# Cross-covariance attention: V in 8 KB rows of eight heads, 1 MB loads, and copies of V's transposes that interleave four blocks

## The chip, the cores and the metric

The kernel runs on one core of a Trainium2 chip. The metric is the device time of one execution in microseconds, the median of several runs. The profile is one execution taken by the hardware profiler; its span is a little shorter than the device time.

A core has a matrix engine (TensorE, in the profile PE, with its weight loads as PEld), three engines for elementwise work (VectorE or DVE, ScalarE or ACT, GpSimd or POOL) and a sync engine (SP), which in this kernel issues all transfers. Sixteen DMA engines carry the transfers between the chip's main memory (HBM) and the on-chip memory of 128 partitions (SBUF). TensorE writes its results into a second on-chip memory, PSUM.

## The reference

```python
# Q, K, V: (batch 8, heads 12, seq 512, dim 64), float32
Q_norm = Q / (np.linalg.norm(Q, axis=-2, keepdims=True) + 1e-10)
K_norm = K / (np.linalg.norm(K, axis=-2, keepdims=True) + 1e-10)
attn = np.einsum('bhnd,bhne->bhde', Q_norm, K_norm)        # 64 x 64 per head
attn = np.exp(attn - np.max(attn, axis=-1, keepdims=True))
attn = attn / (np.sum(attn, axis=-1, keepdims=True) + 1e-10)
return np.einsum('bhnd,bhde->bhne', V, attn).astype(np.float32)
```

There are 96 heads. Each head's Q, K and V are 128 KB, and so is its output; in all 37.7 MB are read and 12.6 MB written. The norms run along the sequence, so a head's attention is a 64 x 64 matrix, and everything about Q and K is had from products along the sequence. V is needed with its sequence along the columns of the weights, that is transposed.

## The kernel before

The heads are cut into 24 units of four heads (`U = 24`), and two units make a pair (`S = 12` pairs). A unit's Q lies in 128 partitions of 16 sequence rows each, so that one partition is a contiguous row of 4 KB in HBM, and 32 partitions are one head. Only the last unit's Q and K have another form, two rows of 2 KB per partition.

```python
D, T, HU, J = 64, 16, 4, 8          # dim, sequence rows per partition, heads per unit, T // 2
TAIL, WIDE, BOTH = S - 1, U - 1, S - 8

Qu = Q.rearrange("b h (p t) d -> (b h p) (t d)", t=T)       # rows of 16 x 64 x 4 B = 4 KB
Ku = K.rearrange("b h (p t) d -> (b h p) (t d)", t=T)
Vu = V.rearrange("b h (p t) d -> (b h p) (t d)", t=T)
Of = out.rearrange("b h n d -> (b h n d)").rearrange("(s r i p x) -> s i p r x", r=2, i=2, p=128, x=J * D)

NB = dict(qk=4, v=4, vb=4, qkb=2, vt=2, so=11, sm=2, ab=4)  # buffers of each pool

def load_qk(u, x):                  # x = 0: Q, 1: K; 512 KB each
    if x == 0:
        qk32[u] = qp.tile([128, 2, T, D], F32, name="qk32")
    if u < WIDE:
        nc.sync.dma_start(out=qk32[u][:, x], in_=(Qu, Ku)[x][u * 128:(u + 1) * 128])
    else:
        ...                         # the last unit, rows of 2 KB
def load_v(u):                      # 512 KB
    v32[u] = vp.tile([128, T, D], F32, name="v32")
    nc.sync.dma_start(out=v32[u], in_=Vu[u * 128:(u + 1) * 128])
def store(s, i, k=None):            # 512 KB, rows of 2 KB; the last one in two halves
    ...
    nc.sync.dma_start(out=o[:, :, rows], in_=so[s, i][:, :, rows])
```

The work on a pair: `cast_qk` turns Q and K to bf16 side by side (`qkb`, always VectorE). `grams` multiplies this with itself on TensorE, which gives both the products of Q and K and, on the diagonal, the squared norms (`gram` in PSUM). `squares` and `sums` take the norms (`scr`, `n`), `cross` copies the product of K and Q (`kq`), `powers` takes 1/norm (`r`), `scale_k` scales the rows (`kqs`), `logits` transposes (`lg`), `exps` takes exponentials with the scale of Q and sums them (`ex`, `esum`), `normalise` divides (`ab`).

V goes another way to the same product: `cast_v` (`vb`), `vtrans` (transposes on TensorE into PSUM, `vps`), `vcopy` (to SBUF, `vt`), and then `outs` multiplies with `ab` into PSUM (`po`), `ocopy` copies to `so`, and `store` writes.

```python
def cast_v(eng, u):
    s, r = divmod(u, 2)
    if r == 0:
        vb[s] = vbp.tile([128, T, 2, D], BF16, name="vb")
    copy(eng, vb[s][:, :, r], v32[u])
def vtrans(s, k, c):                # c is None: both blocks of a half in one PSUM tile, 8 transposes
    ...
    for n, c in enumerate(cs):
        for j in range(J // 2):
            t = J * c + k * (J // 2) + j
            nc.tensor.transpose(ps[:, n, j, :], vb[s][:, t].rearrange("p r d -> p (r d)"), identb)
def vcopy(eng, s, k, c):            # two blocks c interleave: c is the innermost of vt
    if k == 0 and not c:
        vt[s] = vtp.tile([128, J, 128, 2], BF16, name="vt")
    o = vt[s][:, k * (J // 2):(k + 1) * (J // 2)].rearrange("p j x c -> p c j x")
    copy(eng, o if c is None else o[:, c:c + 1], vps[s, k, c])
def outs(s, x):                     # 8 products, weights of 64 columns out of vt
    i, k = divmod(x, 2)
    ...
            w = vt[s][:, k * (J // 2) + j, 32 * h:32 * (h + 1), :].rearrange("p x c -> p (x c)")
            nc.tensor.matmul(po[s, x][e * D:(e + 1) * D, j].rearrange("p r d -> p (r d)"), w, ab[s][:, h, :])
```

The order of the instructions on each engine is fixed when the program is built. A small planner (`Order`) lays out all pieces with estimated costs and ranks, and also chooses between engines where two are named (V's casts, `kq`, `kqs`, and from pair `BOTH` on the copies `vt` and `so`). Its ranks are constants of the kernel:

```python
R = dict(cq=4, gr=3.211, sq=1.1, kq=1.1, rd=5.393, pw=2.74, sc=3, rq=1, lg=1.5, ex=1.5, nm=1.394, cv=5, vt=1.1, vc=4.693, ou=1.326, oc=0.6)
BIAS = dict(sc=-0.3, kq=-0.6, cv=-0.3, vc=1, oc=5)
QK_PACE, V_FROM, V_PACE, ST_LAG = 0.5249, 0.1777, 1.0559, 0.6059
```

The sync engine issues transfers in a fixed order, and one waits until the eighth before it has landed.

Of the kernel before, what the change touches and what calls it, by code (L numbers as in the profile page):

```python
# [13 lines left out]
D = 64  # L14
T = 16
# [87 lines left out]
def kernel(  # L103
# [9 lines left out]
    assert N == 32 * T and Q.shape[3] == D  # L113
    U = B * H // HU
    S = U // 2
    TAIL = S - 1
    WIDE = U - 1
    BOTH = S - 8

    Qu = Q.rearrange("b h (p t) d -> (b h p) (t d)", t=T)
    Ku = K.rearrange("b h (p t) d -> (b h p) (t d)", t=T)
    Vu = V.rearrange("b h (p t) d -> (b h p) (t d)", t=T)

    Qw = Q.rearrange("b h (p j) d -> (b h p j d)", j=J).rearrange("(u m p x) -> u p m x", m=2, p=128, x=J * D)
    Kw = K.rearrange("b h (p j) d -> (b h p j d)", j=J).rearrange("(u m p x) -> u p m x", m=2, p=128, x=J * D)

    Of = out.rearrange("b h n d -> (b h n d)").rearrange("(s r i p x) -> s i p r x", r=2, i=2, p=128, x=J * D)

    ctx.enter_context(tc.manual_schedule())

    NB = dict(qk=4, v=4, vb=4, qkb=2, vt=2, so=11, sm=2, ab=4)
    const = ctx.enter_context(tc.tile_pool(name="const", bufs=1))
    qp = ctx.enter_context(tc.tile_pool(name="qp", bufs=NB["qk"]))
    vp = ctx.enter_context(tc.tile_pool(name="vp", bufs=NB["v"]))
# [20 lines left out]
    def copy(eng, o, i):  # L157
        if eng == "ACT":
            nc.scalar.copy(o, i)  # L159
        elif eng == "DVE":  # L160
            nc.vector.tensor_copy(o, i)  # L161
        else:
            nc.gpsimd.tensor_scalar(out=o, in0=i, scalar1=1.0, scalar2=0.0, op0=ALU.mult, op1=ALU.add)  # L163

    def load_qk(u, x):

        if x == 0:
            qk32[u] = qp.tile([128, 2, T, D], F32, name="qk32")
        if u < WIDE:
            nc.sync.dma_start(out=qk32[u][:, x], in_=(Qu, Ku)[x][u * 128:(u + 1) * 128])  # L170
        else:
            nc.sync.dma_start(out=qk32[u][:, x].rearrange("p (m j) d -> p m (j d)", m=2), in_=(Qw, Kw)[x][u])

    def load_v(u):
        v32[u] = vp.tile([128, T, D], F32, name="v32")
        nc.sync.dma_start(out=v32[u], in_=Vu[u * 128:(u + 1) * 128])

    def store(s, i, k=None):
        rows = slice(None) if k is None else slice(k * (J // 2), (k + 1) * (J // 2))
        o = Of[s, i].rearrange("p r (j d) -> p r j d", d=D)  # L180
        nc.sync.dma_start(out=o[:, :, rows], in_=so[s, i][:, :, rows])

    def cast_qk(u, x):
        if x == 0:
            qkb[u] = qkp.tile([128, T, 2 * D], BF16, name="qkb")
        nc.vector.tensor_copy(qkb[u][:, :, x * D:(x + 1) * D], qk32[u][:, x])  # L186

    def cast_v(eng, u):

        s, r = divmod(u, 2)  # L190
        if r == 0:
            vb[s] = vbp.tile([128, T, 2, D], BF16, name="vb")
        copy(eng, vb[s][:, :, r], v32[u])

    def grams(u):

# [69 lines left out]
                out=a[half, :, half], in0=e[half], in1=ri[half, :, None].to_broadcast([D, HU, D]), op=ALU.mult,  # L266
            )

    def vtrans(s, k, c):

        cs = range(2) if c is None else (c,)
        if c is None:
            ps = vps[s, k, c] = ps_v.tile([128, 2, J // 2, 128], BF16, name="vps")
        else:
            ps = vps[s, k, c] = late_pool().tile([128, 1, J // 2, 128], BF16, name="vps")
        for n, c in enumerate(cs):
            for j in range(J // 2):
                t = J * c + k * (J // 2) + j
                nc.tensor.transpose(ps[:, n, j, :], vb[s][:, t].rearrange("p r d -> p (r d)"), identb)  # L279

    def vcopy(eng, s, k, c):
        if k == 0 and not c:
            vt[s] = vtp.tile([128, J, 128, 2], BF16, name="vt")
        o = vt[s][:, k * (J // 2):(k + 1) * (J // 2)].rearrange("p j x c -> p c j x")
        copy(eng, o if c is None else o[:, c:c + 1], vps[s, k, c])

    def outs(s, x):
        i, k = divmod(x, 2)
        po[s, x] = ps_o.tile([128, J // 2, 2, D], F32, name="po")
        for j in range(J // 2):  # L290
            for e in range(2):
                h = 2 * i + e
                w = vt[s][:, k * (J // 2) + j, 32 * h:32 * (h + 1), :].rearrange("p x c -> p (x c)")
                nc.tensor.matmul(po[s, x][e * D:(e + 1) * D, j].rearrange("p r d -> p (r d)"), w, ab[s][:, h, :])  # L294

    def ocopy(eng, s, x):
        i, k = divmod(x, 2)
# [25 lines left out]

    plan = Order(size)
    X = 1.29
    R = dict(cq=4, gr=3.211, sq=1.1, kq=1.1, rd=5.393, pw=2.74, sc=3, rq=1, lg=1.5, ex=1.5, nm=1.394, cv=5, vt=1.1, vc=4.693, ou=1.326, oc=0.6)
    BIAS = dict(sc=-0.3, kq=-0.6, cv=-0.3, vc=1, oc=5)
    QK_PACE, V_FROM, V_PACE, ST_LAG = 0.5249, 0.1777, 1.0559, 0.6059

    def vt_end(s):  # L330
        return ("vt", s, 1, 1 if s >= TAIL else None) if s >= 0 else None

    def v_at(v):
        return V_FROM + V_PACE * v / U
# [7 lines left out]
    def back(kind, i, n, *rest):  # L342
        return (kind, i - n, *rest) if i - n >= 0 else None

    for u in range(U):
        s, r = divmod(u, 2)
        at = QK_PACE * u / U
        free = [back("cq", u, NB["qk"], 0), back("cq", u, NB["qk"], 1)]
        piece(("lq", u), {"DMA": X}, free, [back("lk", u, 1)], at, load_qk, u, 0)
        piece(("lk", u), {"DMA": X}, free, [("lq", u)], at, load_qk, u, 1)  # L350
        piece(("cq", u, 0), {"DVE": 0.72}, [("lq", u), back("gr", u, NB["qkb"])], [back("cq", u, 1, 1)], R["cq"] + 0.01 * u, cast_qk, u, 0)
        piece(("cq", u, 1), {"DVE": 0.72}, [("lk", u)], [("cq", u, 0)], R["cq"] + 0.01 * u, cast_qk, u, 1)
        piece(("gr", u), {"PE": 1.6}, [("cq", u, 0), ("cq", u, 1), back("kq", s, 1)], [back("gr", u, 1)], R["gr"] + 0.01 * u, grams, u)
    for s in range(S):
        SM = NB["sm"]
# [8 lines left out]
        piece(("lg", s), {"PE": 0.6}, [("sc", s), back("ex", s, 1)], [], R["lg"] + 0.01 * s, logits, s)  # L364
        piece(("ex", s), {"ACT": 1.30}, [("lg", s), ("rq", s), back("nm", s, NB["sm"])], [], R["ex"] + 0.01 * s, exps, s)
        piece(("nm", s), {"DVE": 1.12}, [("ex", s)] + [back("ou", s, NB["ab"], x) for x in range(4)], [], R["nm"] + 0.01 * s, normalise, s)
    for v in range(U):
        s = v // 2
        piece(("lv", v), {"DMA": X}, [back("cv", v, NB["v"])], [back("lv", v, 1)], v_at(v), load_v, v)
        piece(("cv", v), {"POOL": 1.15, "DVE": (0.72, BIAS["cv"])} if s >= BOTH else {"POOL": 1.15},  # L370
              [("lv", v), vt_end(v // 2 - NB["vb"])], [back("cv", v, 1)], R["cv"] + 0.01 * v, cast_v, v)
    for s in range(S):
        t = s >= TAIL
        halves = [(k, c) for k in range(2) for c in ((0, 1) if t else (None,))]
        for n, (k, c) in enumerate(halves):
            if not t:
                wait = [("vc", s, 0, None) if k else back("vc", s, 1, 1, None)]
            else:
                wait = [("vc", s - 1, k, c) if s > TAIL else ("kq", S - 1)]
            order = [("vt", s, *halves[n - 1]) if n else ("vt", s - 1, 1, 1 if s > TAIL else None) if s else None]  # L380
            piece(("vt", s, k, c), {"PE": 0.6 if t else 0.8}, [("cv", 2 * s), ("cv", 2 * s + 1)] + wait, order, R["vt"] + 0.01 * s, vtrans, s, k, c)
            order = [("vc", s, *halves[n - 1])] if n else []
            copies = {"ACT": 0.74 if t else 1.31}
            if s >= BOTH:
                copies["DVE"] = (0.74 if t else 1.42, BIAS["vc"])
            piece(("vc", s, k, c), copies, [("vt", s, k, c)] + [back("ou", s, NB["vt"], x) for x in range(4)], order, R["vc"] + 0.01 * s, vcopy, s, k, c)
        for x in range(4):
            i, k = divmod(x, 2)
            n = 4 * s + x - 2
            wait = [("oc", n // 4, n % 4)] if n >= 0 else []  # L390
            order = [("ou", s, x - 1) if x else back("ou", s, 1, 3)]
            piece(("ou", s, x), {"PE": 0.5}, [("vc", s, *h) for h in halves if h[0] == k] + [("nm", s)] + wait, order, R["ou"] + 0.01 * s, outs, s, x)
            n = 2 * s + i - NB["so"]
            free = [("st", n // 2, n % 2)] if k == 0 and n >= 0 else []
            order = [("oc", s, x - 1) if x else back("oc", s, 1, 3)]
            piece(("oc", s, x), {"ACT": 0.6, "DVE": (0.68, BIAS["oc"])} if s >= BOTH else {"ACT": 0.6}, [("ou", s, x)] + free, order, R["oc"] + 0.01 * s, ocopy, s, x)
        for i in range(2):
            order = [("st", s, 0) if i else back("st", s, 1, 1)]
            if (s, i) == (S - 1, 1):

                piece(("sh", s, i), {"DMA": 0.67}, [("oc", s, 2)], order, v_at(2 * s + i) + ST_LAG, store, s, i, 0)
                piece(("st", s, i), {"DMA": 0.67}, [("oc", s, 3)], [("sh", s, i)], v_at(2 * s + i) + ST_LAG, store, s, i, 1)
            else:
                piece(("st", s, i), {"DMA": X}, [("oc", s, 2 * i), ("oc", s, 2 * i + 1)], order, v_at(2 * s + i) + ST_LAG, store, s, i)
# [32 lines left out]
```

## Time and profile before

| | before |
|---|---|
| median of 3 runs | 131.9 us (131.63 to 132.55) |
| span of the profile | 129.5 us |
| transfers issued by the sync engine | 97 (72 loads, 25 stores) |
| busy, VectorE | 94.6 us (73%) |
| busy, TensorE | 78.1 us (60%) |
| busy, ScalarE | 76.8 us (59%) |
| busy, GpSimd | 29.0 us (22%) |

The profile page lists the busy time of each engine, a row of 40 slices for each (a digit is the busy tenth of a slice of 3.2 us, 9 is 90% or more), the DMA queues with their packets, a chain of waits followed back from the last instruction, and the groups of instructions with their mean durations. A line number such as L186 is that of the kernel. "SPq" is the sync engine's queue; a wait such as `SPq L170 <- DMA v<-in_V_dram: 11.5, 13, 1.3` means that issues of line 170 waited 11.5 us in 13 cases, at most 1.3 us, until that transfer had landed.

### The profile page before, as it was taken

Reading aid. Unit: us, or ns where it says so; the run is one execution under the profiler, and the core shown is the slowest. Engines: PE = TensorE matmul, PEld = TensorE weight load, DVE = VectorE, ACT = ScalarE, POOL = GpSimd, SP = SyncE. Lnnn points to the kernel's source line nnn. Section 1 sums busy time; section 2 is a strip of 40 time slices with the busy share of each in tenths; the row PEclk is TensorE's granted clock in tenths of the full one; section 3 lists DMA queues with packets and bytes.
Section 4 is the critical chain, followed back from the end, with each engine's and each line's share of the span. In section 5 each row is a group of like instructions: output and inputs, shape, how many; then the busy total and the mean of one; then the engine's idle time right before and its main releaser. Section 6 shows DMA issues by size and latency. Waiting matters only on the chain.

```text
span 129.5 us, 4929 instructions
## 1 busy us (share of the span) xinstructions
PE 78.1 (60%) x2128; PEld 64.4 (50%) x2128; DVE 94.6 (73%) x148; ACT 76.8 (59%) x218; POOL 29.0 (22%) x33
## 2 busy tenths in 40 slices
PE   0055665955369676864399863596774876678000
PEld 0045654844358464653288752585563765466000
DVE  3445859699898589999938999969999969761000
ACT  3000226690279589994387979168879499598100
POOL 3000090506301191312342033003423030300000
PEclk9999999999955899999756999559999599655555
DMA  3999999999999999999999999999999999999982
GB/s 133 382 410 424 405 412 406 409 406 409 406 410 409 406 406 401 415 402 410 404 403 416 411 414 407 423 409 406 404 413 407 416 397 414 403 405 407 409 331 79
DMA packets 17444, 50.63 MB, mean 391 GB/s; under 512 B 1552, under 2 KB 2064, under 8 KB 17424
## 3 DMA queue, kind: packets, MB, share of 16 engines
q1 hardware_dynamic: 17424, 50.34, 98.3%
q8 instruction: 16, 0.26, 0.8%
q14 instruction: 4, 0.03, 0.1%
HBM read 37.75 MB, written 12.58 MB: 389 GB/s over the span
## 4 chain that ended last, share of the span: by engine, by line
DVE 36%; PE 25%; issue 10%; DMA 9%; ACT 7%; SPq 3%; POOL 2%; ACTq 0%
DVE qkb L186 14%; PE gram L207 12%; DMA v<-in_V_dram 9%; DVE scr L214 8%; PE po L294 7%; PE vps L279 6%; DVE ab L265 5%; DVE kq L161 4%; ACT vt L159 4%; SPq L170 3%; DVE n L226 2%; ACT so L159 2%; DVE vb L161 2%; POOL vb L163 2%; ACT ex L256 1%
## 5 line engine op out<-in xcount | busy, mean ns | idle before, releaser
L207 PE MATMUL gram<-qkb 32*128 32x128 bf16 (+1 forms) x1504 | 34.6, 252 | 23.5 <-DVE qkb L186 12.6
L186 DVE CAST qkb<-qk 128x1024 bf16<-128x1024 f32 x48 | 36.3, 781 | 11.0 <-DMA qk<-in_Q_dram 4.6
L207 PEld LDWEIGHTS <-qkb 32*128 32x128 bf16 (+1 forms) x1504 | 29.4, 113 | 26.1 <-DVE qkb L186 13.4
L159 ACT COPY vt<-vps 128x1024 bf16<-128x1024 bf16 (+1 forms) x23 | 29.1, 1272 | 11.6 <-PE vps L279 11.4
L159 ACT COPY so<-po 128x512 f32<-128x512 f32 x48 | 27.0, 609 | 4.9 <-PE po L294 4.6
L294 PE MATMUL po<-ab,vt 128*64 128x128 bf16 x384 | 22.1, 261 | 6.2 <-ACT so L159 3.5
L163 POOL TENSOR_SCALAR vb<-v 128x1024 bf16<-128x1024 f32 x14 | 15.3, 1095 | 45.4 <-DMA v<-in_V_dram 38.3
L279 PE MATMUL vps<-identb,vb 128*128 128x128 bf16 x192 | 18.7, 255 | 10.6 <-ACT vt L159 4.6
L294 PEld LDWEIGHTS <-vt 128*64 128x64 bf16 x384 | 15.9, 133 | 12.6 <-issue 7.7
L279 PEld LDWEIGHTS <-vb 128*128 128x128 bf16 x192 | 14.6, 114 | 13.4 <-issue 9.6
L214 DVE SCALAR_TENSOR_TENSOR scr<-gram,eye 64x512 f32<-64x512 f32 x24 | 16.5, 689 | 5.9 <-PE gram L207 5.5
L237 POOL TENSOR_TENSOR kqs<-kq,r 64x512 f32<-64x512 f32 x11 | 12.4, 1127 | 36.0 <-ACT r L233 32.3
L256 ACT ACTIVATE ex<-lg,rq 128x64 f32<-128x64 f32 x48 | 14.7, 338 | 2.3 <-PE lg L250 2.3
L265 DVE TENSOR_TENSOR ab<-ex,rinv 64x256 bf16<-64x256 f32 x24 | 14.6, 606 | 0.6
L256 ACT ACTIVATION_READ_ACCUMULATOR ex<-lg,rq 128x1 f32 x48 | 11.0, 229 | 0.0
L159 ACT COPY kq<-gram 64x512 f32<-64x512 f32 x2 | 1.2, 582 | 14.6 <-DVE scr L214 14.6
L161 DVE CAST vb<-v 128x1024 bf16<-128x1024 f32 x10 | 7.5, 761 | 1.3 <-DMA v<-in_V_dram 1.2
L226 DVE TENSOR_REDUCE n<-scr 128x8 f32<-128x512 f32 x12 | 8.1, 679 | 0.1
L232 ACT ACTIVATE ln<-n 128x8 f32<-128x8 f32 x12 | 2.8, 237 | 8.6 <-DVE n L226 8.5
L250 PE MATMUL lg<-eye,kqs 64*128 64x64 f32 x48 | 6.4, 265 | 1.6 <-POOL kqs L237 1.6
L161 DVE COPY kq<-gram 64x512 f32<-64x512 f32 x10 | 6.9, 694 | 0.3
L250 PEld LDWEIGHTS lg<-eye,kqs 64*128 64x128 f32 x48 | 4.6, 162 | 3.3 <-POOL kqs L237 2.2
(16 smaller groups left out, 16.5 us busy)
## 6 DMA issues: line engine op xcount, KB each, us to landing
qk<-in_Q_dram SPq DMA_DIRECT2D x24, 512.0 KB, 10.1
qk<-in_K_dram SPq DMA_DIRECT2D x24, 512.0 KB, 10.2
v<-in_V_dram SPq DMA_DIRECT2D x24, 512.0 KB, 10.1
out_dram<-so SPq DMA_DIRECT2D x23, 512.0 KB, 10.1
out_dram<-so SPq DMA_DIRECT2D x2, 256.0 KB, 7.4
```

What stands on the lines that cost most here:

```text
L159: nc.scalar.copy(o, i)
L161: nc.vector.tensor_copy(o, i)
L163: nc.gpsimd.tensor_scalar(out=o, in0=i, scalar1=1.0, scalar2=0.0, op0=ALU.mult, op1=ALU.add)
L186: nc.vector.tensor_copy(qkb[u][:, :, x * D:(x + 1) * D], qk32[u][:, x])
L207: nc.tensor.matmul(gram[s][:, h, r, 0], x, x, start=(t == 0), stop=(t == (T if u < WIDE else J) - 1))
L214: nc.vector.scalar_tensor_tensor(out=scr[s][half], in0=gram[s][half, :, :, 0, half].rearrange("p h r d -> p (h r) d"), scalar=1e-20, in1=e ...
L237: (nc.vector if eng == "DVE" else nc.gpsimd).tensor_tensor(out=kqs[s][HI], in0=kq[s][HI], in1=r8[s][HI, :, None].to_broadcast([D, 2 * HU, ...
L250: nc.tensor.transpose(l[:, h, :], kqs[s][HI, 2 * h:2 * h + 2].rearrange("p r d -> p (r d)"), eye2[HI])
L256: nc.scalar.activation(e[:, h, :], lg[s][:, h, :], AF.Exp, scale=rq[s][:, h:h + 1], accum_out=z[:, h:h + 1])
L265: nc.vector.tensor_tensor(out=a[half, :, half], in0=e[half], in1=ri[half, :, None].to_broadcast([D, HU, D]), op=ALU.mult,)
L279: nc.tensor.transpose(ps[:, n, j, :], vb[s][:, t].rearrange("p r d -> p (r d)"), identb)
L294: nc.tensor.matmul(po[s, x][e * D:(e + 1) * D, j].rearrange("p r d -> p (r d)"), w, ab[s][:, h, :])
```

## The change

V is no longer loaded by unit, in 4 KB rows, but in transfers of 1 MB whose partitions are rows of 32 sequence rows, 8 KB each: 16 partitions are one head, so 128 partitions are eight heads. Two such transfers give the V of two pairs, called `w` here (`W = 6`). A partition then has four blocks of eight sequence rows instead of two, and the copy of the transposes interleaves four blocks, which leaves the output in the same 2 KB rows as before. To match V, a pair's two units are now every other unit of the four that belong to one `w`.

Q and K of pairs 3 to 10 are loaded in one transfer of 1 MB each, in rows of 4 KB as before; pairs 0 to 2 and 11 keep 512 KB. The last V transfer is split into two halves of 512 KB (rows of 4 KB). The aim is fewer and larger packets and fewer transfers. The buffers are cut accordingly (Q and K: 3 of two units; V: 3 of 1 MB; `so`: 13), and the planner's constants are new, so that the order on every engine and the choice between engines differ too.

```diff
-    TAIL = S - 1
+    W = S // 2
+    TAIL = 2
     WIDE = U - 1
+    ONE = 3
...
-    Qu = Q.rearrange("b h (p t) d -> (b h p) (t d)", t=T)
-    Ku = K.rearrange("b h (p t) d -> (b h p) (t d)", t=T)
-    Vu = V.rearrange("b h (p t) d -> (b h p) (t d)", t=T)
+    Qu = Q.rearrange("b h (p t) d -> (b h p) (t d)", t=T).rearrange("(w r e p) x -> w e p r x", r=2, e=2, p=128)
+    Ku = K.rearrange("b h (p t) d -> (b h p) (t d)", t=T).rearrange("(w r e p) x -> w e p r x", r=2, e=2, p=128)
+    Vu = V.rearrange("b h (p t) d -> (b h p) (t d)", t=2 * T).rearrange("(w r p) x -> w r p x", r=2, p=128)
...
-    NB = dict(qk=4, v=4, vb=4, qkb=2, vt=2, so=11, sm=2, ab=4)
+    NB = dict(qk=3, v=3, vb=2, qkb=2, vt=2, so=13, sm=2, ab=4)
...
+    def load_qk(s, x, r):
+        w, e = divmod(s, 2)
+        if s not in qk32:
+            qk32[s] = qp.tile([128, 2, 2, T, D], F32, name="qk32")
+        if 2 * s + (r or 0) >= WIDE:
+            ...                                     # the last unit, as before
+        elif r is None:                             # both units of a pair: 1 MB
+            nc.sync.dma_start(out=qk32[s][:, x].rearrange("p r t d -> p r (t d)"), in_=(Qu, Ku)[x][w, e])
         else:
+            nc.sync.dma_start(out=qk32[s][:, x, r].rearrange("p t d -> p (t d)"), in_=(Qu, Ku)[x][w, e, :, r])
+    def load_v(w, r, c):
+        if (w, r) not in v32:
+            v32[w, r] = vp.tile([128, 2, T * D], F32, name="v32")
+        o, i = v32[w, r], Vu[w, r].rearrange("p (c x) -> p c x", c=2)
+        if c is None:                               # 1 MB, rows of 8 KB
+            nc.sync.dma_start(out=o.rearrange("p c x -> p (c x)"), in_=Vu[w, r])
+        else:                                       # the last one, in halves
+            nc.sync.dma_start(out=o[:, c], in_=i[:, c])
...
+    def vtrans(w, q, f):
+        js = range(2 * q, 2 * q + 2) if f is None else (2 * q + f,)
+        ...
+        ps = vps[w, q, f] = pool.tile([128, 4, len(js), 128], BF16, name="vps")
+        for n, j in enumerate(js):
+            for c in range(4):
+                nc.tensor.transpose(ps[:, c, n, :], vb[w][:, J * c + j].rearrange("p r d -> p (r d)"), identb)
+    def vcopy(eng, w, q, f):
+        if w not in vt:
+            vt[w] = vtp.tile([128, J, 128, 4], BF16, name="vt")
+        o = vt[w][:, 2 * q:2 * q + 2] if f is None else vt[w][:, 2 * q + f:2 * q + f + 1]
+        copy(eng, o, vps[w, q, f].rearrange("p c j x -> p j x c"))
     def outs(s, x):
...
-                w = vt[s][:, k * (J // 2) + j, 32 * h:32 * (h + 1), :].rearrange("p x c -> p (x c)")
+                x16 = slice(16 * (4 * half + h), 16 * (4 * half + h + 1))
+                v = vt[w][:, k * (J // 2) + j, x16, :].rearrange("p x c -> p (x c)")
...
-    R = dict(cq=4, gr=3.211, sq=1.1, kq=1.1, rd=5.393, pw=2.74, sc=3, rq=1, lg=1.5, ex=1.5, nm=1.394, cv=5, vt=1.1, vc=4.693, ou=1.326, oc=0.6)
-    BIAS = dict(sc=-0.3, kq=-0.6, cv=-0.3, vc=1, oc=5)
-    QK_PACE, V_FROM, V_PACE, ST_LAG = 0.5249, 0.1777, 1.0559, 0.6059
+    R = dict(cq=2.5, gr=2.471, sq=0.756, kq=1, rd=3.457, pw=3.5, sc=1, rq=1.9, lg=5, ex=1.1, nm=2.545, cv=1.165, vt=0.9, vc=1.1, ou=2, oc=0.9)
+    BIAS = dict(sc=-0.6, kq=5, cv=1, vc=-0.3, oc=0.6)
+    QK_PACE, V_FROM, V_PACE, ST_LAG = 0.631, 0.0377, 0.7486, 1.5133
```

Left out of the diff are the planner's pieces, which name the new transfers, the two casts per V transfer, and the four turns of transposes per `w`; from the third turn of the last `w` on they are halved (`TAIL`).

## The prediction

> **What bounds the kernel now.** I read the slices and the DMA queue table of the page first, then the busy time by stretch, then the sync engine's waits, then the timeline of the tail. The slices say which engine is never idle:
>
> ```profile
> DVE  3445859699898589999938999969999969761000
> ...
> DMA  3999999999999999999999999999999999999982
> GB/s 133 382 410 424 405 412 406 409 406 409 406 410 409 406 406 401 415 402 410 404 403 416 411 414 407 423 409 406 404 413 407 416 397 414 403 405 407 409 331 79
> DMA packets 17444, 50.63 MB, mean 391 GB/s; under 512 B 1552, under 2 KB 2064, under 8 KB 17424
> ...
> q1 hardware_dynamic: 17424, 50.34, 98.3%
> ```
>
> From the second slice to the 38th the DMA row is solid 9s at about 408 GB/s; VectorE, the busiest engine (94.6 us, 73%), has gaps. The reader is to see one more thing: the rate is the same in pure loading (early) and in pure storing (the end), so the moved bytes and the packets they come in set the time. The chain of waits on the page gives DVE 36% and DMA only 9%; that chain follows buffer dependencies backwards, and is misleading here, because no transfer started late on account of them. The tail shows why:
>
> ```profile
> core 0: us, PE busy (x) PEld busy (x) DVE busy (x) ACT busy (x) POOL busy (x), PEclk, DMA share, GB/s
> ...
> 110.00:116.00 6.00, 4.47 (x50) 3.60 (x48) 4.26 (x8) 4.43 (x15) 1.09 (x1) 0.59 1.05 402
> 116.00:120.00 4.00, 2.85 (x40) 2.19 (x39) 0.88 (x2) 3.36 (x7) 0.00 (x0) 0.50 1.05 407
> 120.00:124.00 4.00, 0.04 (x1) 0.00 (x0) 0.00 (x0) 0.59 (x1) 0.00 (x0) 0.50 1.06 408
> 124.00:126.00 2.00, 0.00 (x0) 0.00 (x0) 0.00 (x0) 0.00 (x0) 0.00 (x0) 0.50 0.82 311
> 126.00:128.00 2.00, 0.00 (x0) 0.00 (x0) 0.00 (x0) 0.00 (x0) 0.00 (x0) 0.50 0.45 158
> ```
>
> Compute ends at 120.7 us (the last copy into `so`), while DMA engines still have work until about 128. The last result waits in the queue behind earlier stores. So compute has some 3 to 4 us of slack at the end. The sync engine's own waits agree:
>
> ```profile
> SPq L170 <- DMA v<-in_V_dram: 11.5, 13, 1.3
> SPq L170 <- DMA qk<-in_Q_dram: 10.7, 11, 1.8
> SPq L176 <- DMA qk<-in_K_dram: 9.1, 9, 2.1
> ...
> SPq L181 <- ACT so L159: 5.9, 5, 2.9
> ```
>
> It mostly waits for an older transfer to land (eight are outstanding at once: each load takes 10.1 us from issue to landing while a new one lands about every 1.28 us), not for a buffer. Only 5.9 us go to waiting for results, at the end, and behind a filled queue.
>
> **What one packet costs.** The trace's packet records of queue 1, grouped by size, have these typical durations: 4 B (the completion write of each transfer, one per engine) 9 ns, 1,024 B 46 ns, 2,048 B 84 ns, 4,096 B 159 ns. From 2 KB to 4 KB is 75 ns for 2,048 B, and 84 - 75 leaves 9 ns per packet. So a packet costs about 9 ns + 37.5 ns per KB, and 1 KB gives 46.5, as measured. Seven of the twelve 8,192 B packets in the trace, all instruction fetches on another queue, took 307 ns; the formula says 309. This is the number that the change rests on.
>
> Per DMA engine (a sixteenth of the packets): 560 of 4 KB x 159 = 89.04 us, 400 of 2 KB x 84 = 33.60, 32 of 1 KB x 46 = 1.47, 97 completions x 9 = 0.87; sum 124.98 us. The queue's first packet to its last is 125.88 us, so the slowest engine is accounted for within 0.9 us.
>
> [...]512 KB transfers already run at 408 GB/s[...]. I count only the saved completion writes.
> [...]
>
> **The change part by part.**
> 1. V in 8 KB rows. Eleven of its twelve megabytes come in 8 KB packets, 88 per engine instead of 176 of 4 KB; the last megabyte is still loaded in two halves of 4 KB rows. 88 x (2 x 159 - 309) = 0.79 us per engine saved, all on the path.
> 2. Fewer transfers. Counted from the changed kernel's instruction order: V 13 transfers instead of 24; Q and K 32 instead of 48 (pairs 3 to 10 in 1 MB, but still rows of 4 KB); stores 25 as before. 70 instead of 97: 27 x 9 ns = 0.24 us.
> 3. The sum per engine is 384 x 159 + 400 x 84 + 32 x 46 + 88 x 309 + 70 x 9 = 123.95 us, 1.03 us less than 124.98. Start and end have the same form: Q and K of unit 0 still come first in 512 KB, and the last two stores are still 256 KB.
> 4. Work moved between engines, by the instruction orders and the mean durations of before. VectorE: 5 fewer casts of V x 761 ns, 10 fewer `kq` x 694, one `kqs` less x 690, against 4 more `vt` of 1,024 x 1,302, one half of 733 and 3 `so` (estimated at the 694 of a like `kq` copy): about -3.4 us. ScalarE: 10 more `kq` x 582, 4 fewer `vt` x 1,318, a half of 788, 3 fewer `so` x 609: about -2.1 us. GpSimd: 5 casts x 1,095 and one `kqs` x 1,127 more: +6.6 us on an engine 22% busy. None of this is on the DMA path; it makes compute a little lighter, so the slack at the end should live.
> 5. The copy of V's transposes writes four adjacent values instead of every second, and reads across four blocks. No row of the trace before has this pattern. Even 20% either way of 29 us is 6 us spread over 115 us beside a full queue.
> 6. Buffers. Q and K: 3 of two units instead of 4 of one, V: 3 of 1 MB instead of 4 of 0.5; `so` 13 instead of 11. With eight transfers outstanding, now up to 1 MB each, loads are queued earlier.
>
> **Does the queue stay full?** I walked through the new issue order, landing 512 KB per 1.28 us, 1 MB of Q or K per 2.56 and 1 MB of V per 2.48 from 3.05 us on. A typical tight load, Q of pair 10, may begin at about 80 us; its buffer was filled by 61.5 us, which gives its casts 17 us. The last V lands at about 101 us instead of 110, the last K at about 98 instead of 95, because more stores are left to the end: 18 of 512 KB and two halves. The last store but two begins at about 122.5 us. The last pair's chain (cast, Gram, norms, exponentials, product, copies) took 25.7 us from the landing of the last K before (issued at 84.8, 10.2 to land: 95.0, to 120.7); the last V was in the way until 110. If it takes 18 to 23 now, compute ends at 116 to 121: in time, with less to spare.
>
> **The rivals.**
> - A: no gain from 8 KB rows (the engine splits them, or HBM gives them more slowly). Then only 0.24 us is won: 131.7 us. Against it: the 307 ns of the instruction fetches; for it: those come by another queue.
> - B: the tail becomes the bound. Stores are deferred more (18 instead of 14 after the last load), and K lands 3 us later. If compute ends at 123 or 124 instead of 121, the queue runs dry before the last stores: 132 to 134 us. For it: ScalarE's last nine copies go hand in hand with TensorE at half clock. Against: V comes 9 us sooner, and VectorE and ScalarE have less to do.
> - C: starving in the middle because a buffer of two units comes free only when all four casts are done. One gap of 2 us gives 133. Against it: the 17 us above, and the deeper queue in bytes.
> - D: compute now lags less, and the tail tightens too, since engines finishing at different times (124 to 128 us) even out with fewer packets: 130.
>
> **Range and chances.** 131.9 - 1.03 = 130.9 us. A and a little of B go up to 132.8, D and a faster start down to 129.8. Faster by over 2% needs 129.3, 2.6 us, more than twice what packets can give: 0.07. Slower by over 2% needs a real gap: 0.08. Within 2%: 0.85.
>
> **What would show it right or wrong.** Right: 15,584 packets on queue 1, GB/s in pure loading at about 414 (two megabytes at 16 x 159 + 9 ns per engine to one at 8 x 309 + 9, against 409 at 4 KB alone), a DMA row of 9s to slice 38, queue 1 about 1 us shorter. An 8 KB packet well over 309 ns, or 16,992 packets, means A. A slice below 9 before the last two means C, and which issue waited then says for which buffer; DMA share below 1 from 115 us on with the sync engine waiting for `so` means B.

## The result and the profile after

The changed kernel takes 130.63 us in the median of four runs (130.39 to 130.86), the kernel before 132.01 us (131.63 to 132.55). The ratio is 0.9892, with a 95% interval of 0.985 to 0.9935: 1.4 us less, within 0.9 to 2.0. The prediction was 130.9 us, a ratio of 0.992.

From the page of the changed kernel, VectorE, the DMA row, the transfer rate by slice, the packets, and two DMA queues:

```profile
DVE  3444649849999389699986798997999799830000
...
DMA  4999999999999999999999999999999999999982
GB/s 133 389 430 410 432 399 409 408 416 409 422 406 411 404 408 410 402 413 430 410 414 406 416 415 418 405 420 415 405 410 403 405 399 406 402 407 406 408 312 75
DMA packets 15605, 50.64 MB, mean 392 GB/s; under 512 B 1120, under 2 KB 1632, under 8 KB 14176
...
q1 hardware_dynamic: 15584, 50.34, 98.0%
q8 instruction: 16, 0.26, 0.8%
```

The packets of queue 1 are exactly the 15,584 counted. In the trace the 1,408 packets of 8,192 B took 312 ns in the median (309 most often, 314 on average), and the 4 KB packets beside them 159 (163.5 on average): two of 4 KB cost 6 to 13 ns more than one of 8 KB, where the prediction had 9. The DMA row is still solid: the coarser buffers never let the queue run dry. Queue 8, which stood on the page of before with the same numbers, becomes important below.

By stretch (columns as before: length, the busy time of five engines with their instructions, TensorE's clock, DMA share, GB/s), one stretch of pure loading and the tail:

```profile
20.00:30.00 10.00, 7.49 (x172) 5.99 (x172) 7.73 (x11) 5.19 (x10) 2.95 (x3) 1.00 1.03 413
...
110.00:116.00 6.00, 3.67 (x60) 3.05 (x61) 3.45 (x9) 5.16 (x18) 0.73 (x1) 0.69 1.05 403
116.00:120.00 4.00, 0.79 (x14) 0.52 (x10) 0.00 (x0) 1.18 (x3) 0.00 (x0) 0.50 1.06 409
...
124.00:126.00 2.00, 0.00 (x0) 0.00 (x0) 0.00 (x0) 0.00 (x0) 0.00 (x0) 0.50 0.67 250
126.00:128.00 2.00, 0.00 (x0) 0.00 (x0) 0.00 (x0) 0.00 (x0) 0.00 (x0) 0.50 0.29 102
```

The kernel before in the same stretch of pure loading:

```profile
20.00:30.00 10.00, 6.37 (x176) 5.21 (x173) 8.72 (x14) 6.79 (x20) 2.09 (x2) 1.00 1.02 407
```

The prediction had 414 and 409. Compute ends at 117.4 us (before: 120.7), the sync engine's last issue at 120.5, while the DMA engines finish one by one between 124 and 128. So the time still belongs to the DMA engines, and to the last of them in particular.

The copies of V's transposes and V's casts on VectorE (mean ns after the comma) changed their cost:

```profile
L164 ACT COPY vt<-vps 128x1024 bf16<-128x1024 bf16 x17 | 17.2, 1012 | 16.9 <-PE vps L289 16.8
...
L166 DVE CAST vb<-v 128x1024 bf16<-128x1024 f32 x5 | 5.1, 1012 | 0.9 <-DMA v<-in_V_dram 0.9
```

The same two groups in the kernel before:

```profile
L159 ACT COPY vt<-vps 128x1024 bf16<-128x1024 bf16 x21 | 27.7, 1318 | 11.6 <-PE vps L279 11.4
...
L161 DVE CAST vb<-v 128x1024 bf16<-128x1024 f32 x10 | 7.5, 761 | 1.3 <-DMA v<-in_V_dram 1.2
```

### The profile page after: what moved, and what is told of

The parts are those of the page before. It is cut to its first block, busy times and chain, and to the rows that moved or that the text cites. A ratio compares the mean times of both kernels' runs of the same rounds, so it can differ in the third digit from the quotient of the medians.

```text
span 129.1 us, 4881 instructions
## 1 busy us (share of the span) xinstructions
PE 77.8 (60%) x2128; PEld 63.3 (49%) x2128; DVE 91.0 (71%) x140; ACT 72.5 (56%) x220; POOL 37.3 (29%) x39
## 3 DMA queue, kind: packets, MB, share of 16 engines
q1 hardware_dynamic: 15584, 50.34, 98.0%
## 4 chain that ended last, share of the span: by engine, by line
DMA 50%; DVE 16%; PE 10%; ACT 8%; issue 3%; SPq 1%; POOL 1%; ACTq 0%; POOLq 0%; DVEq 0%
DMA qk<-in_K_dram 21%; DMA v<-in_V_dram 15%; DMA qk<-in_Q_dram 14%; DVE qkb L200 7%; PE gram L220 6%; ACT so L164 3%; DVE scr L227 3%; DVE vt L166 2%; PE po L306 2%; DVE ab L278 2%; PE vps L289 2%; ACT ex L269 2%; ACT vt L164 2%; DVE n L239 1%; SPq L180 1%
## 5 line engine op out<-in xcount | busy, mean ns | idle before, releaser
L220 PE MATMUL gram<-qkb 32*128 32x128 bf16 (+1 forms) x1504 | 36.6, 259 | 21.7 <-DVE qkb L200 15.4
L168 POOL TENSOR_SCALAR vb<-v 128x1024 bf16<-128x1024 f32 x19 | 21.9, 1162 | 46.7 <-DMA v<-in_V_dram 46.4
L164 ACT COPY so<-po 128x512 f32<-128x512 f32 x45 | 25.0, 592 | 7.6 <-PE po L306 7.5
L164 ACT COPY vt<-vps 128x1024 bf16<-128x1024 bf16 (+1 forms) x18 | 17.8, 987 | 16.9 <-PE vps L289 16.8
L289 PE MATMUL vps<-identb,vb 128*128 128x128 bf16 x192 | 16.7, 236 | 6.6 <-POOL vb L168 3.9
L289 PEld LDWEIGHTS <-vb 128*128 128x128 bf16 x192 | 12.6, 105 | 9.6 <-POOL vb L168 4.9
L164 ACT COPY kq<-gram 64x512 f32<-64x512 f32 x12 | 7.0, 581 | 14.4 <-DVE scr L227 14.0
L166 DVE COPY vt<-vps 128x1024 bf16<-128x1024 bf16 (+1 forms) x8 | 7.9, 1019 | 0.1
L166 DVE CAST vb<-v 128x1024 bf16<-128x1024 f32 x5 | 5.1, 1012 | 0.9 <-DMA v<-in_V_dram 0.9
L275 DVE RECIPROCAL rinv<-esum 128x4 f32<-128x4 f32 x12 | 2.1, 171 | 2.5 <-ACT ex L269 2.5
```

The lines of the kernel that those rows point to most:

```text
L220: nc.tensor.matmul(gram[s][:, h, r, 0], x, x, start=(t == 0), stop=(t == (T if u < WIDE else J) - 1))
L289: nc.tensor.transpose(ps[:, c, n, :], vb[w][:, J * c + j].rearrange("p r d -> p (r d)"), identb)
```

## Experiments

Each variant starts from the changed kernel unless it says otherwise. Ratios are to the kernel before in the same comparison, on the same chip. The difference of two variants is the difference of their ratios, times 132.0 us. The changed kernel itself was timed four times only, and its interval (0.985 to 0.9935) goes into every difference to it: these are good to some 0.7 us either way.

**1. V in 4 KB packets, transfers still of 1 MB.** A pad in the SBUF tile breaks each row in two, and V's casts read around it; nothing else differs, not even the order of the instructions.

```diff
-            v32[w, r] = vp.tile([128, 2, T * D], F32, name="v32")
+            v32[w, r] = vp.tile([128, 2, T * D + 8], F32, name="v32")
...
-            nc.sync.dma_start(out=o.rearrange("p c x -> p (c x)"), in_=Vu[w, r])
+            nc.sync.dma_start(out=o, in_=i)          # o, i: two runs of 4 KB per partition
...
```

> The changed kernel with V still in 1 MB transfers and in the same order, but the V tile in SBUF is padded between its two halves, so that a partition's row goes in two packets of 4 KB instead of one of 8 KB; all engines' instructions are the same. Packet theory: 88 packets of 309 ns per DMA engine become 176 of 159 ns, 0.79 us more, 131.4 us (ratio to before about 0.995), and 16,992 packets. Rival 'the larger transfers brought the gain' and rival 'the new order of the engines brought it': no change, 130.6 us (0.989).

Measured: 131.29 us, ratio 0.9956 (0.9936 to 0.9976). Against the changed kernel's 0.9892 that is 0.0064, 0.84 us; the packet law said 0.79. Queue 1 carries the 16,992 packets expected:

```profile
q1 hardware_dynamic: 16992, 50.34, 98.1%
```

**2. V in 2 KB packets, transfers still of 1 MB.**

```diff
-            v32[w, r] = vp.tile([128, 2, T * D], F32, name="v32")
+            v32[w, r] = vp.tile([128, 2, 2, T * D // 2 + 8], F32, name="v32")
...
```

> The same with three pads, four packets of 2 KB for each V row. Packet theory: 352 packets of 84 ns instead of 88 of 309 per engine, 2.38 us more, 133.0 us (ratio to before about 1.007), that is slower than the kernel before although transfers and order are the changed kernel's. Rivals of large transfers or of the order: 130.6 us.

Measured: 132.88 us, ratio 1.0076 (1.0047 to 1.0106). 0.0184 above the changed kernel, 2.43 us; the law said 2.38. With transfers, order and buffers of the changed kernel, it is slower than the kernel before. From its page:

```profile
DMA packets 20085, 50.64 MB, mean 386 GB/s; under 512 B 1120, under 2 KB 1632, under 8 KB 20064
```

The bytes and the completion writes (under 512 B) are those of the changed kernel; the rest is packets. Run 2 against run 1, which leaves the changed kernel's interval out, is 0.0120, 1.58 us, good to about 0.5; the law said 1.59. Runs 1 and 2 settle what the 8 KB rows do, and rule out for this part that the larger transfers or the new order brought it.

**3. V in transfers of 512 KB with 4 KB rows.**

```diff
-            nc.sync.dma_start(out=o.rearrange("p c x -> p (c x)"), in_=Vu[w, r])
+            for c in range(2):
+                nc.sync.dma_start(out=o[:, c], in_=i[:, c])
```

> The changed kernel with every 1 MB transfer of V issued as two of 512 KB with 4 KB rows (one half of the row each), as in the kernel before; order of the other engines as in the changed one. Packet theory: 0.79 us for the packets and 11 more completion writes of 9 ns, 131.5 us. Rival 'size of the transfers': clearly above the padded 1 MB variant, by more than 0.3 us.

Measured: 132.19 us, ratio 1.003 (1.001 to 1.005), 0.9 us slower than run 1 with the same packets. My theory allowed 0.1. Its profile has a dip early on, by stretch:

```profile
7.00:8.00 1.00, 0.96 (x36) 0.69 (x28) 0.34 (x1) 0.00 (x0) 0.00 (x0) 1.00 1.13 369
8.00:9.00 1.00, 0.00 (x0) 0.00 (x0) 0.43 (x2) 0.00 (x0) 0.00 (x0) 1.00 0.99 246
9.00:10.00 1.00, 0.33 (x16) 0.33 (x20) 0.62 (x1) 0.00 (x0) 0.00 (x0) 1.00 0.87 287
```

The last columns are to be read together: the DMA share stays at 0.87 to 0.99 while the rate falls to 246 GB/s, so most engines were busy with packets that took longer, not waiting for work. But the dip alone does not place the loss. Run 1, whose V goes in 1 MB transfers, has one too, in the second slice of its page (274 GB/s from 4 to 5 us and 221 from 5 to 6):

```profile
GB/s 160 300 408 421 412 416 411 402 410 406 410 405 419 400 408 402 405 415 420 408 416 407 411 417 408 410 406 413 405 413 401 406 399 407 400 407 406 411 327 79
```

The profiled executions of runs 5 and 8 have it as well (305 and 328 GB/s in the second slice), those of the kernel before and of the changed kernel have not (382 and 389).

**4. The same, but the first two V transfers as in the changed kernel.**

```diff
+            if w == 0:
+                nc.sync.dma_start(out=o.rearrange("p c x -> p (c x)"), in_=Vu[w, r])
+            else:
+                for c in range(2):
+                    nc.sync.dma_start(out=o[:, c], in_=i[:, c])
```

> The variant with V in transfers of 512 KB and 4 KB rows, but the first two V transfers (the first group of 16 heads) stay 1 MB in 8 KB rows as in the changed kernel. Theory that 512 KB transfers of V lose only at the start, where their packets were slow in the profile (242 to 270 GB/s in the 7th and 8th us of the queue): 131.4 us, as with the padded 1 MB transfers (ratio 0.995). Rival 'half the bytes outstanding, or rows in halves, cost all along': 132.1 us (1.002).

Measured: 131.10 us, ratio 0.9967 (0.9944 to 0.9989). Of run 3's 1.003, 0.0063 is gone, 0.83 us, although only two of V's twelve transfers differ, and those account for 16 of 88 packet pairs, 0.14 us. So most of the loss of run 3 comes with the form of these first two transfers. Why they cost so much in halves was not found: half rows and fewer bytes in flight at the start were not told apart.

**5. Q and K of the middle pairs in 512 KB.**

```diff
-            nc.sync.dma_start(out=qk32[s][:, x].rearrange("p r t d -> p r (t d)"), in_=(Qu, Ku)[x][w, e])
+            for q in range(2):
+                nc.sync.dma_start(out=qk32[s][:, x, q].rearrange("p t d -> p (t d)"), in_=(Qu, Ku)[x][w, e, :, q])
```

> The changed kernel with Q and K of the middle pairs in two transfers of 512 KB instead of one of 1 MB; rows of 4 KB either way. Packet theory: 16 more completion writes of 9 ns, 0.14 us, 130.8 us, within the noise of the changed kernel. Rival 'size of the transfers': 0.5 us or more, 131.1 us or above.

Measured: 130.76 us, ratio 0.9932 (0.9906 to 0.9958). The interval meets that of the changed kernel (up to 0.9935). Inconclusive: the absolute time, 0.1 us above the changed kernel's, fits the packet theory, and the ratio, 0.0040 or 0.5 us above it with 0.7 either way, the rival.

**6. Useless work on ScalarE in the last chain.**

```diff
+        if (s, x) == (S - 1, 0):
+            for _ in range(5):
+                nc.scalar.copy(spare, qk32[S - 1][:, 0, 0].rearrange("p t d -> p (t d)")[:, :512])
```

> The changed kernel with five copies of 128x512 more on ScalarE ahead of the last pair's first copy to so, some 3 us of useless work in the last chain; the output is the same. Theory that the DMA queue sets the end: compute ends at about 120.4 instead of 117.4 us, the last stores were issued at 119 to 120.5 anyway, no change beyond 0.3 us: 130.6 us. Rival 'the tail is bound by compute': 133.5 us.

Measured: 130.56 us, ratio 0.9898 (0.9861 to 0.9935): no change. From its timeline (start, length, engine, instruction):

```profile
114.18 3.23 ACT L315 COPY spare<-qk 128x512 f32<-128x512 f32 x5
117.31 1.06 ACT L164 COPY so<-po 128x512 f32<-128x512 f32 x2
...
118.62 1.07 ACT L164 COPY so<-po 128x512 f32<-128x512 f32 x2 [0.24 <-PE po L306]
```

3.2 us of work that nobody needs, and nothing comes of it; compute ends at 119.7 us in place of 117.4. Compute's last chain has slack, as the prediction said.

**7. The small packets that were left, made large.**

```diff
-    WIDE = U - 1
+    WIDE = U                                   # last unit: Q and K in 4 KB rows
-        return (0, 1) if s < ONE or s == S - 1 else (None,)
+        return (0, 1) if s < ONE else (None,)  # last pair: 1 MB
-            halves = (0, 1) if (w, r) == (W - 1, 1) else (None,)
+            halves = (None,)                   # last V: 8 KB rows
-            if (s, i) == (S - 1, 1):
+            if False:                          # last store: one of 512 KB
```

> The changed kernel with the small packets that are left made large: the last V transfer whole in 8 KB rows, the last store whole in 2 KB rows, Q and K of the last unit in 4 KB rows, Q and K of the last pair in 1 MB. Packet theory: per engine 0.08 + 0.14 + 0.14 us less, 130.3 us, since compute ended at 117.4 us while the queue was full until 122. Rival 'the tail is compute-bound': the later last V and the whole last store cost, 131 us or more.

Measured: 131.37 us, ratio 0.9969 (0.9948 to 0.9991), a miss of over 1 us. Queue 1 carried 14,880 packets, as the new forms ask for. What differed unasked: the last unit's other form needs 64 more instructions on TensorE (32 more products, each with its weight load), and queue 8 showed 17 fetches instead of 16, the last one at 120.6 us on the transfers' own time scale (from their first packet).

**8. 64 more instructions on TensorE, nothing else.**

```diff
     for emit, eng in plan.run():
         emit(eng)
+    extra = late_pool().tile([128, 4, 1, 128], BF16, name="vps")
+    for n in range(32):
+        nc.tensor.transpose(extra[:, n % 4, 0, :], identb, identb)
```

> The changed kernel with 32 useless transposes (64 instructions) behind TensorE's last product; nothing else differs, nobody waits for them, the output is the same. Fetch theory (from the trim run): the instruction queue shows 17 fetches of 16 KB instead of 16, the last at about 120 us, it goes through one of the DMA engines that the transfers use and delays this one by some 1.5 us, so that the end comes about 1.2 us later: 131.8 us (ratio to before about 0.998). Rival 'trim was slow because its last V or last store was whole': TensorE is done with them by about 119 us, no change, 130.6 us (0.989).

Measured: 131.55 us, ratio 1.0003 (0.9981 to 1.0025): 0.0111 above the changed kernel, 1.46 us (0.8 to 2.1), for work that nobody waits for. The rows of queues 1 and 8 of its page, and of its timeline the useless work:

```profile
q1 hardware_dynamic: 15584, 50.34, 96.7%
q8 instruction: 17, 0.28, 0.8%
```

```profile
117.91 3.24 PE L443 MATMUL vps<-identb 128*128 128x128 bf16 x32
```

The transfers are the same to the packet, and TensorE is done at 121.2 us, long before the end. The seventeenth fetch is the change. The trace also has sixteen completion marks for each transfer, one per DMA engine; the time from a transfer's first mark to its last tells how far the engines have come apart (transfers counted from 0):

```
transfer number       3    15    33    48    60    63    69
transfers alone     1.13  1.12  1.08  1.17  1.21  1.20  1.17 us
changed kernel      0.92  1.90  3.36  3.92  3.98  4.00  3.97 us
64 more on TensorE  1.39  2.70  4.04  4.11  4.06  5.54  5.38 us
```

Without compute the engines keep the distance they got at the start. In the changed kernel they drift apart in steps, as one fetch after the other falls on some of them: when the first one is carried, at 11.3 us from the first packet, one mark goes from about 0.4 to 1.9 us behind the first, and the others stay; at the second, at 19.9 us, another goes from 0.3 to 1.9. In the last row the step from 4.06 to 5.54 us comes between transfers 60 and 63, when the seventeenth fetch is carried (from 119.6 us): 1.5 us on one engine, which was one of the last already; the other fifteen marks stay here too. Run 7's trace has the same step, from 3.83 to 5.14 us on one engine, at the first transfer to land after its fetch at 120.6 us. In numbers: take 0.0111 for its seventeenth fetch from its 0.9969 and 0.986 is left, where 0.987 had been expected. That subtraction is an argument; the variant without the extra instructions wasn't tried.

In the changed kernel the first fetch came after 256 of TensorE's products and weight loads and the sixteenth after 4,120, one for 258 on average, with some 140 to 360 between one and the next. 64 more are a quarter of that average; here they brought another fetch.

**9 and 10. The transfers alone.** All compute is left out, and the stores write zeros instead of the result; the order of the transfers is that of the changed kernel and that of the kernel before.

```diff
-    for emit, eng in plan.run():
-        emit(eng)
+    plan.run()
+    ...                                        # so[s, i] = one tile of zeros for all
+    for _, _, key, eng in plan.order:
+        if key[0] in ("lq", "lk", "lv", "st", "sh"):
+            plan.pieces[key][4](eng)
```

> The changed kernel's transfers in their order with no compute at all (stores write zeros, the output is left wrong): the floor of the transfers. Theory that the queue alone sets the time: at most 0.5 us below the changed kernel, 130.2 us. Rival 'compute holds the queue back': 128 us or less.

> The kernel before's 97 transfers in their order with no compute (stores write zeros, the output is left wrong). Packet theory: at most 0.5 us below the kernel before, and 1.03 us above the changed kernel's transfers alone.

Measured: 128.63 us for the changed order, 129.10 us for the old one, ratios 0.9745 (0.9705 to 0.9785) and 0.9801 (0.9766 to 0.9836). Both lie some 2 to 2.7 us below their kernels, not 0.5. From the first packet to the last it was 123.53 us against 124.67, 1.14 less; the sums of the prediction were 123.95 and 124.98. That 1.14 is close to the 1.03 foreseen in part by luck: in this execution of the old order the engines were already 1.67 us apart at transfer 3, in that of the new one 1.13, and in device time the two orders differ by 0.5 us only (0.7 by the ratios, with 0.7 either way). So the packet sums come within 0.4 us of the transfers without compute; they are not the time of the queue beside it. From the page of the changed order:

```profile
q1 hardware_dynamic: 15584, 50.34, 99.3%
q14 instruction: 1, 0.01, 0.0%
```

There is no queue 8 here, in a program without compute: none of that queue's sixteen fetches is left. On average over the sixteen engines the last completion mark comes 1.36 us later in the changed kernel than in its transfers alone, about one step of run 8 per engine, and the very last mark 2.5 us later, as the steps fall unevenly. But these two variants leave out all other compute along with the fetches: that the fetches make up the whole 2 to 2.7 us is argued, not shown.

**11. The output in rows of 4 KB.**

```diff
-            for e in range(2):
-                h = 2 * i + e
+            for h in range(HU):
...
-                nc.tensor.matmul(po[s, x][e * D:(e + 1) * D, j].rearrange("p r d -> p (r d)"), v, ab[s][:, h, :])
+                nc.tensor.matmul(po[s, x][32 * h:32 * (h + 1), j].rearrange("p r d -> p (r d)"), v, ab[s][:, h, :])
```

> The changed kernel with the output in rows of 4 KB: a partition holds 16 sequence rows of a head, four heads fill the 128 partitions, so a product has weights of 32 columns and there are 768 of them instead of 384; stores are 1 MB (the last pair's two of 512 KB in 2 KB rows); copies of V's transposes interleave two blocks. The planner's ranks are not fitted to it. Packet theory: 11 pairs x (32 x 84 + 18 - 16 x 2 x 159 / 2 - 9) ns = 1.68 us less per engine, 129.0 us. Rival: TensorE, with 384 products of some 60 ns more (about 23 us on 78), becomes the bound or delays the tail: 132 us or more.

Measured: 144.72 us, ratio 1.0926 (1.0862 to 1.0989). The rival's outcome came. Its slices, one wait of the sync engine, and the group of the products:

```profile
GB/s 173 350 406 419 422 409 406 416 412 412 421 404 409 406 419 406 424 417 411 417 414 416 407 414 420 417 416 409 403 411 292 30 284 307 11 115 398 79 366 221
...
L304 PE MATMUL po<-ab,vt 128*32 128x128 bf16 x768 | 25.2, 287 | 15.7 <-ACT so L164 6.8
```

```profile
SPq L194 <- ACT so L164: 35.1, 9, 13.5
```

From slice 31 on the queue runs dry and stores wait 35 us for results. 768 products instead of 384, stores that become ready only 1 MB at a time, and 19 fetches: which of these held up the results was not taken apart. The planner's ranks were not fitted to it, so this speaks of this version, not of 4 KB stores as such.

**12. The copies by themselves.** Eight copies of 128x1024 bf16 from PSUM to SBUF in each of five patterns, nothing of the computation.

```diff
+        eng(plain, ps)
+        eng(two_w.rearrange("p j x c -> p c j x"), two)    # before: write steps by two
+        eng(two_r, two.rearrange("p c j x -> p j x c"))    # read across blocks
+        eng(four_w.rearrange("p j x c -> p c j x"), four)
+        eng(four_r, four.rearrange("p c j x -> p j x c"))  # changed kernel
```

> Nothing of the computation: eight copies each of 128x1024 bf16 from PSUM to SBUF on ScalarE and then on VectorE, in five patterns: plain; two blocks interleaved with the write stepping by two (the kernel before); the same with the read stepping across blocks and the write contiguous; four blocks interleaved, write stepping by four; four blocks, read across blocks, write contiguous (the changed kernel). Theory 'a write of 2-byte values with a step costs ScalarE': 1.3 us for both stepping writes, 1.0 us for the other three. Rival 'interleaving four instead of two matters': both patterns of two 1.3 us, both of four 1.0 us.

```profile
L58 ACT COPY four_w<-ps 128x1024 bf16<-128x1024 bf16 x8 | 19.4, 2421 | 0.2
...
L54 ACT COPY two_w<-ps 128x1024 bf16<-128x1024 bf16 x8 | 10.3, 1292 | 0.2
...
L60 DVE COPY four_r<-ps 128x1024 bf16<-128x1024 bf16 x8 | 9.8, 1226 | 0.2
...
L60 ACT COPY four_r<-ps 128x1024 bf16<-128x1024 bf16 x8 | 8.2, 1024 | 0.2
L56 ACT COPY two_r<-ps 128x1024 bf16<-128x1024 bf16 x8 | 8.1, 1012 | 0.2
L52 ACT COPY plain<-ps 128x1024 bf16<-128x1024 bf16 x8 | 8.1, 1012 | 1.0 <-PE ps L43 0.8
L52 DVE COPY plain<-ps 128x1024 bf16<-128x1024 bf16 x8 | 5.5, 691 | 56.2 <-ACT four_r L60 56.0
```

On ScalarE the stepping write is what costs, not the number of blocks: reading across two or four blocks and writing contiguously takes 1,012 and 1,024 ns, as long as a plain copy (1,012). I had not expected the 2,421 ns of a step of four. The changed kernel's faster copy comes from the side that steps, and two blocks would have had it too.

## Why the prediction held

- What bounds the kernel: right. Run 6 puts 3.2 us into compute's last chain and nothing changes; the changed kernel has no slice that starves. But the queue is not free of compute: without it the same transfers take 2.0 us less (run 9).
- The packet law, 9 ns and 37.5 ns per KB: right, on both sides of 4 KB. 0.84 us measured for 0.79 (run 1) and 2.43 for 2.38 (run 2), each with some 0.7 us either way, and 1.58 for 1.59 between the two, with 0.5. That they meet within 0.05 us is closer than the measurements are good for. One reading behind it was off: of the twelve packets of 8,192 B in the trace of before, six took 307 ns, not seven, and a seventh 309. The 312 ns of V's own packets are what counts.
- 27 completion writes less, 0.24 us: not resolved. After the 0.84 us of the packets, 0.58 us of the measured 1.42 (0.0044 of the ratio) remain, 0.3 to 0.8 by run 1's interval, for fewer transfers, start, order and everything else; run 5 was inconclusive.
- Queue 1 about 1 us shorter: not seen in the two kernels' profiles (125.88 us from first to last packet before, 126.00 after, in executions of 131.28 and 130.86 us), seen in the transfers alone. What did fall is the time that the packets of queue 1 took: the records add up to 127.3 us per engine before and 126.4 after, 0.9 less. The engines' coming apart (4.0 us at the end after, 3.5 before) and the spread between executions of one kernel, over a microsecond in most comparisons above, hide it in the time from first packet to last.
- "The slowest engine is accounted for within 0.9 us": the number was right, the reading incomplete. The sum leaves out the instruction fetches of queue 8: sixteen of about 1.05 us, one per engine on average. The prediction read the fetches of queue 14 for the time of an 8 KB packet and passed over the row of queue 8 on the same page. The number of fetches is the same in both kernels; the difference of the two therefore came out right, and run 7, where it isn't, went wrong by the size of one fetch.
- Load on the engines: VectorE -3.6 us for -3.4 predicted, though its casts of V took 1,012 ns and not 761. ScalarE -4.2 for -2.1, mostly from the copies of V, which took 1,012 ns and not 1,318. GpSimd +8.3 for +6.6. Compute's end at 117.4 us was inside 116 to 121. The 14 stores that the prediction counts after the last load of before include the two halves; on that count there are 20 now, not 18.
- Rival A is refuted by the 312 ns and by runs 1 and 2, B by run 6, C by the DMA row. D, a gain beyond the packets, stays possible: 1.4 us measured for 1.03, but the interval, 0.9 to 2.0, holds both.

## What to carry to other kernels

Where all DMA engines are busy from start to end, count packets: sum each size's typical duration over a sixteenth of the packets. In runs 1 and 2 the effect of the row length came out as this sum said (0.84 us for 0.79, 2.43 for 2.38), as far as half a microsecond can be told. Then look at the rows of the instruction queues as well: in these traces the fetches ran on the same engines (run 8's seventeenth put one engine's mark 1.5 us back) and the slowest engine set the end, so 64 instructions that nobody waits for cost 1.46 us (0.8 to 2.1), of the order of what larger packets for eleven megabytes bring (0.84). When interleaving blocks of bf16 in a copy from PSUM to SBUF, try the form in which the read steps and the write runs contiguously: for four blocks it took 1,024 ns on ScalarE and 1,226 on VectorE in run 12, the stepping write 2,421 and 2,419.

## What the runs showed of the hardware that was not expected

- TensorE's instruction fetches: 16 of 16 KB, about 1.05 us each, for 4,256 products and weight loads; 17 for 4,320; 19 for 5,024. One more delayed one DMA engine by some 1.5 us and the kernel by 1.46 us, 0.8 to 2.1 (run 8). The spread of the engines at the end was 4.0 us beside compute and 1.2 us without.
- Engines that lost time in the first microseconds did not catch up: without compute (run 9) their spread was 1.13 us at transfer 3 and 1.17 us at transfer 69.
- bf16 copies of 1,024 values from PSUM: on ScalarE 1,012 ns plain, 1,292 with a write step of two, 2,421 with four; on VectorE 691 ns plain, 1,226 reading across four blocks, and 1,290 and 2,419 with stepping writes.
- The first two megabytes of V in halves of rows cost some 0.8 us (runs 3 and 4); the cause is open. In some executions the rate dips in the first 10 us whatever the form of V, to 221 to 287 GB/s for a microsecond or two at a DMA share of 0.74 to 0.99 (runs 1, 3, 5 and 8). Whether these dips are what sets executions of one kernel apart is not shown.
